# Attention stage of a hybrid encoder block: a hand-written pipeline of 100 slots on TensorE, ScalarE and VectorE, and keys' second halves copied by DMA

## The chip, the cores and the metric

The kernel runs on one core of a Trainium2 chip. A core has five engines that each work through their own queue: TensorE (PE; its weight loads are shown apart as PEld), VectorE (DVE), ScalarE (ACT), GpSimd (POOL) and SyncE (SP), which here issues nearly all DMAs. The metric is the device time of one execution in microseconds, lower is better. Three runs of the kernel before gave 1541.37, 1541.6 and 1543.32 us, median 1541.6 us.

## The reference, cut to what matters

One encoder block on 1024 positions of width 1024, all in float32:

```python
h = rmsnorm(x, g_mix) * (1 + scale1) + shift1
qa, ka, va, qb, kb, vb, ga, gb = split(h @ w_in)       # 6 x 512, 2 x 1024 columns
oa = mixture_of_dilations(qa, ka, va, rel_bias)        # 8 heads of 64, dilations 1, 4, 16
ob = neighbourhood_attention_2d(qb, kb, vb, na_rpb)    # 8 heads of 64, 16 x 64 grid, window 8 x 16
x = x + gate1 * ((sigmoid(ga) * (oa @ w_branch_dil) + sigmoid(gb) * (ob @ w_branch_na)) @ w_out)
h2 = rmsnorm(x, g_ffn) * (1 + scale2) + shift2
u_val, u_gate = split(depthwise_conv_seq(h2 @ w_up, conv_w, conv_b))
y = rmsnorm(x + gate2 * ((gelu(u_gate) * u_val) @ w_down), g_final)
```

Each attention is softmax(q k^T / 8 + bias) v with a window. In the dilated one, the three patterns are merged by their softmax denominators: the kernel computes a "near" pattern (dilation 1) and a "far" one (dilations 4 and 16 together, with the log of 2 where both apply) and weighs the two outputs per position.

## The kernel before, in words

**Stages.** The beginning (0 to about 160 us of the profile) makes `h`, the values of both branches and the adaLN sums. The attention stage (about 160 to 675 us) is the one that the change rewrites. Then follow the branch and output products (to about 860 us), the feed-forward up products (to about 1305 us) and down products (to the end).

**Splitting.** Float32 precision comes from splitting each operand into a high and a low part; a product of 512 columns over one block of 128 rows is three matmuls (`product`, L83 to L85: high x high, high x low, low x high). A weight tile of 128x1024 is loaded into `wraw` (`w_load`, L64), and `split` writes its high part on ACT (L56) and its low part on POOL (L60).

**Tiles of the attention stage.** 30 weight tiles are multiplied with `h`, each in two halves of 512 columns and 8 blocks of rows: 7 of queries, 7 of keys (the first pair's were done earlier) and 16 gate tiles. Each half lands in a PSUM bank `pj` (two buffers). Queries are evicted by `q_half` (L317 ACT, L318 DVE), keys by `k_half`: for each of the pair's two heads `i`, ACT writes the high part `ks` to the head's 64 partitions (L351), DVE the low part `kl` (L352), then ACT writes the high part a second time, to the other 64 partitions (L353), and POOL copies the low part there (L354). `gate_tile` evicts on ACT (L797) and writes to DRAM (`g_scr`, L798).

**Attention.** `attend_dil` takes a pair of heads: per head four far steps and four near steps of scores in PSUM `S` (two banks), a softmax (`softmax`: L606 DVE adds the bias and takes the maximum, L607 ACT exponent and sum), four transposes into PSUM `T` (two banks; L629, L667), a split of it into `th` and `tl` (L611 ACT, L612 DVE), and the product with the values into PSUM `O` (two banks; L636, L682), evicted by `finish_o` (L576, L577). After both heads follow the merging factors: 32 copies of a few elements on DVE (L692, L709), a spread of the factors to 128x512 on ACT (L713), transposes (L717) and the weighing (L719). `attend_na` does four column blocks per head: scores (L748), softmax (L752, L754), a normalisation on POOL and DVE (L759), transposes (L769), splits (L772, L773), products with the values (L781) and evictions (L787, L788). The results go to DRAM (`o_scr`, L724 and L789) and are read back by the next stage (`o_operands`, L842).

**What sets the order.** In this stage the program says only what is computed, pair after pair, with the next pair's projections and some gate tiles after each. A scheduler that runs a timeline of the engines at build time sets the order of every queue from that. Elsewhere `tc.manual_schedule(engines=...)` fixes the order of the named engines' instructions to the program's order; instructions outside of such a block can still be placed between them. The beginning up to the loads of the first two heads stands in such a block for all engines (SP's queue too), with the first pair's queries and keys made by a generator `qk_steps`; the stage after attention stands in another.

Of the kernel before, what the change touches and what calls it, by code (L numbers as in the profile page):

```python
# [28 lines left out]
def hybrid_encoder(tc, xT, c, w_ada, small, w_in, p1_bias, p23_bias, na_bias, ln2_mult, ident, w_br, w_out,  # L29
# [62 lines left out]
    qkpool = tc.alloc_tile_pool(name="qk", bufs=3)  # L92
# [29 lines left out]
    homes = iter([(qkpool, "kl", 3)] + [(qkpool, n, b) for n, b in (("qs", 3), ("ks", 3), ("qb", 2))  # L122
# [173 lines left out]
    def qk_steps(br, pr, ws=None, ps=None):  # L296
        qt, kt = ((0, 4), (12, 16))[br]
        qs = [qkpool.tile([128, S], FR, name="qs") for _ in range(2)]
        ks = [qkpool.tile([128, S], FR, name="ks") for _ in range(2)]
        kl = [qkpool.tile([128, S], FR, name="kl") for _ in range(2)]  # L300
        qb = []

        def q_half(hf, w, p=None):
            cols = halves[hf]
            if p is None:
                p = ps_g.tile([128, 512], FT, name="pj")
                if br == 0:
                    product(p, w, lambda k: h[hf, k])
                else:
                    q_windows(p, w, hf)  # L310
            for i in range(2):
                a, b = slice(64 * i, 64 * i + 64), slice(64 - 64 * i, 128 - 64 * i)
                d, pp = qs[i][:, cols], p
                if br:
                    d = qs[i].rearrange("p (v r t) -> p v r t", v=64, r=4)[:, :, 2 * hf:2 * hf + 2]
                    pp = p.rearrange("p (r v t) -> p v r t", r=2, v=64)
                act.activation(d[a], pp[a], AF.Copy)  # L317
                dve.tensor_tensor(d[b], pp[a], f(d[a]), OP.subtract)  # L318

        def q_windows(p, w, hf):  # L320

            whi, wlo = w
            for k in range(KT):
                mhi, mlo = (t.rearrange("p (r w c t) -> p r c w t", r=2, w=16, c=4) for t in h[hf, k])
                for x, (ww, m) in enumerate(((whi, mhi), (whi, mlo), (wlo, mhi))):
                    for r in range(2):
                        pe.matmul(p[:, 256 * r:256 * r + 256], ww[:, k], m[:, r], start=k + x + r == 0,
                                  stop=k == KT - 1 and x == 2, skip_group_check=True)

        def q_blocks():  # L330
            for i in range(2):
                q = qkpool.tile([128, S], FR, name="qb", bufs=2)
                for r in range(4):
                    pool.tensor_scalar(q.rearrange("p (b r j) -> p r b j", b=8, r=4)[:, r],
                                       f(qs[i][:, 256 * r:256 * r + 256]).rearrange("p (b j) -> p b j", b=8), 1.0, None,
                                       OP.mult)
                qb.append(q)

        def k_half(hf, w, p=None):
            cols = halves[hf]  # L340
            if p is None:
                p = ps_g.tile([128, 512], FT, name="pj")
                product(p, w, lambda k: h[hf, k])
            for i in range(2):
                a, b = slice(64 * i, 64 * i + 64), slice(64 - 64 * i, 128 - 64 * i)
                kh, ll, pp = ks[i][:, cols], kl[i][:, cols], p
                if br:
# [7 lines left out]

        if ws:
            for hf in range(2):
                yield
                if hf:
                    ps = [ps_g.tile([128, 512], FT, name="pj") for _ in range(2)]  # L360
                    for k in range(KT):
# [1151 lines left out]
```

## Time and profile before

| | us |
|---|---|
| median of three runs | 1541.6 |
| the profiled execution's own time | 1546.68 |
| its span, first to last instruction | 1544.9 |

The profile is of one execution, on the core's own clock. Its page gives the busy time of each engine, the span in 40 slices and the costliest groups; its views answer for a stretch of time ("windows"), for what an engine waited for ("waits"), or list the instructions in order of time ("timeline"). A matmul's row gives a start and a modelled duration; matmuls overlap, so that the distance from one start to the next is what one costs, and the busy share of PE says only where PE had nothing at all in flight. An "idle before" with an arrow names the instruction that ended the wait. SPq is SP's queue.

### The profile page before, as it was taken

The page shows a single profiled execution, that of the slowest core. Times are in us where ns is not written, and L with a number is a line of the kernel's source. Part 1 is how long each engine was busy: PE and PEld are TensorE (multiplying, and loading weights), DVE is VectorE, ACT ScalarE, POOL GpSimd, SP SyncE. Part 2 cuts the span into 40 slices and gives each one's busy share as a digit, 9 for nine tenths or more (in the row PEclk, how much of TensorE's full clock was granted, in tenths as well). Part 3 has the DMA queues.
Part 4 walks back from the last instruction along what each step waited for, and adds up shares of the span by engine and source line. Part 5 has one row for each costly group of instructions (what it writes and reads, how often), then busy time and mean ns, then how long its engine had stood idle before and what let it go on. Part 6 is the DMA issues. An engine that isn't in the chain of part 4 may idle for free. (4 is left out here: it accounts for less than half of the span.)

```text
span 1544.9 us, 21706 instructions
## 1 busy us (share of the span) xinstructions
PE 1502.2 (97%) x7740; PEld 1277.8 (83%) x7740; DVE 1005.9 (65%) x1884; ACT 802.1 (52%) x1440; POOL 815.6 (53%) x648
## 2 busy tenths in 40 slices
PE   8999999999999999999999898999999998999998
PEld 7988888888898898878888677888888887878787
DVE  6676457765766665536515898766666667787765
ACT  4331567675866767543345444444444447476442
POOL 1014355353537657312267678767777665778711
PEclk9999999999999999999999999999999999999998
DMA  9467232223534344467644112222222224513313
GB/s 349 174 255 249 67 93 66 89 74 88 159 97 134 117 140 136 156 207 230 205 152 153 49 69 96 82 82 83 84 88 88 84 79 166 200 52 134 105 55 110
DMA packets 108597, 196.86 MB, mean 127 GB/s; under 512 B 39716, under 2 KB 52388, under 8 KB 108452
## 3 DMA queue, kind: packets, MB, share of 16 engines
q1 hardware_dynamic: 108216, 195.20, 38.3%
q8 instruction: 61, 1.00, 0.3%
q14 instruction: 48, 0.39, 0.1%
q10 hardware_dynamic: 272, 0.26, 0.1%
HBM read 158.73 MB, written 42.47 MB: 130 GB/s over the span
## 5 line engine op out<-in xcount | busy, mean ns | idle before, releaser
L60 POOL TENSOR_TENSOR wlo<-wraw,whi 128x512 fp32r<-128x512 f32 (+1 forms) x154 | 193.4, 1277 | 247.1 <-ACT whi L56 234.6
L83 PE MATMUL pj<-h,whi 128*128 128x512 f32 x448 | 179.8, 401 | 3.8 <-ACT ks L353 1.8
L84 PE MATMUL pj<-h,whi 128*128 128x512 f32 x448 | 178.9, 399 | 1.6 <-DVE h L208 1.6
L85 PE MATMUL pj<-h,wlo 128*128 128x512 f32 x448 | 178.0, 397 | 0.0
L60 POOL TENSOR_TENSOR wsl<-big,wsh 128x512 fp32r<-128x512 f32 (+1 forms) x90 | 123.6, 1394 | 50.9 <-ACT wsh L56 50.9
L56 ACT ACTIVATE whi<-wraw 128x1024 fp32r<-128x1024 f32 (+2 forms) x81 | 81.1, 1002 | 81.9 <-PE pj L84 32.5
L354 POOL TENSOR_SCALAR kl<-kl 64x512 fp32r<-64x512 f32 x32 | 64.1, 2002 | 96.9 <-DVE kl L352 95.8
L1171 DVE SCALAR_TENSOR_TENSOR big<-wc,sm,big 128x256 f32<-128x256 f32 (+1 forms) x132 | 103.2, 830 | 16.8 <-ACT big L1165 16.6
L83 PEld LDWEIGHTS pj<-h,whi 128*128 128x128 f32 x448 | 84.9, 190 | 19.6 <-ACT ks L353 2.3
L606 DVE CUSTOM_DVE_ANT_0 P<-S,bias 128x256 f32<-128x256 f32 x128 | 52.0, 422 | 74.7 <-PE S L653 50.2
L84 PEld LDWEIGHTS pj<-h,whi 128*128 128x128 f32 x448 | 84.9, 190 | 17.0 <-DVE h L208 2.9
L85 PEld LDWEIGHTS pj<-h,wlo 128*128 128x128 f32 x448 | 84.9, 189 | 15.1
L607 ACT ACTIVATE P<-P,st 128x256 f32<-128x256 f32 x128 | 64.3, 503 | 40.0 <-DVE st L606 39.5
L1171 DVE SCALAR_TENSOR_TENSOR big<-pj,sm,big 128x512 f32<-128x512 f32 x132 | 67.1, 564 | 16.4 <-ACT big L1165 16.4
L60 POOL TENSOR_TENSOR wsl<-wraw,wsh 128x384 fp32r<-128x384 f32 (+1 forms) x46 | 53.8, 1190 | 44.8 <-ACT wsh L56 44.7
L1165 ACT ACTIVATE big<-wc,sm 128x512 f32<-128x512 f32 x44 | 35.8, 815 | 74.0 <-DVE wc L989 42.7
L563 POOL TENSOR_TENSOR vv<-vv 96x256 fp32r<-96x256 f32 (+2 forms) x32 | 41.0, 1289 | 59.2 <-ACT vv L562 54.6
L759 POOL TENSOR_SCALAR P<-P,stb 128x288 f32<-128x288 f32 (+1 forms) x32 | 39.2, 1226 | 48.0 <-DVE stb L756 41.1
L56 ACT ACTIVATE wsh<-big 128x1024 fp32r<-128x1024 f32 (+1 forms) x45 | 44.7, 997 | 37.2 <-POOL big L941 21.5
L1197 ACT ACTIVATE big<-big 128x1024 f32<-128x1024 f32 x22 | 23.3, 1060 | 74.6 <-DVE big L1171 74.6
L994 DVE TENSOR_TENSOR pj<-pj,wc 128x512 f32<-128x512 f32 x34 | 23.6, 695 | 58.3 <-PE pj L978 58.3
L612 DVE TENSOR_TENSOR tl<-T,th 128x512 fp32r<-128x512 f32 x64 | 43.9, 689 | 10.8 <-ACT th L611 10.1
(397 smaller groups left out, 4904.2 us busy)
## 6 DMA issues: line engine op xcount, KB each, us to landing
wraw<-w_in SPq DMA_DIRECT2D x34, 512.0 KB, 4.0
wada<-w_ada SPq DMA_DIRECT2D x31, 512.0 KB, 7.8
big<-w_up SPq DMA_DIRECT2D x22, 512.0 KB, 4.7
wraw<-w_up SPq DMA_DIRECT2D x22, 512.0 KB, 3.6
as<-big SPq DMA_DIRECT2D x22, 512.0 KB, 3.0
big<-as SPq DMA_DIRECT2D x22, 512.0 KB, 8.5
wraw<-w_down SPq DMA_DIRECT2D x24, 384.0 KB, 3.6
gs<-gs SPq DMA_DIRECT2D x32, 256.0 KB, 2.0
```

Of the source, the lines that this page charges most:

```text
L56: act.activation(hi, raw, AF.Copy)
L60: lo_eng.tensor_tensor(lo[:, i:i + step], raw[:, i:i + step], f(hi)[:, i:i + step], OP.subtract)
L83: pe.matmul(psum, whi[:, k0 + k], mhi, start=k == 0, stop=False)
L84: pe.matmul(psum, whi[:, k0 + k], mlo, start=False, stop=False)
L85: pe.matmul(psum, wlo[:, k0 + k], mhi, start=False, stop=k == n - 1)
L354: pool.tensor_scalar(ll[b], f(ll[a]), 1.0, None, OP.mult)
L563: pool.tensor_tensor(lo[:m, cs_], f(lo[:m, cs_]), f(vv[:m, cs_, 0:64]), OP.subtract)
L606: dve.tensor_tensor_reduce(pp, d, bias, -1.0, BIG, OP.add, OP.min, mi)
L607: act.activation(pp, pp, AF.Exp, bias=mi, scale=-1.0, accum_out=li)
L612: dve.tensor_tensor(tl, pt, f(th), OP.subtract)
L759: (pool, dve)[R].tensor_scalar(pp, pp, st[:, 1, 2 * cb + R:2 * cb + R + 1], None, OP.mult)
L1171: dve.scalar_tensor_tensor(y[:, dst], src, wt, y[:, dst], OP.mult, OP.add)
```

## The change

The functions `qk_steps`, `attend_dil`, `attend_na` and `gate_tile` go. In their place jobs are put into 101 slots (0 to 100), and one block with the order of PE, ACT and DVE fixed to the program's walks through the slots; POOL and SP are still ordered by the scheduler. A dilated head starts every 8 slots, a pair every 16, a neighbourhood head every 4 slots from slot 64 on. In each slot stand scores of one step, transposes of an earlier step and products with the values of a still earlier one, and between them `fill(n)` puts steps of the projections and gates (three matmuls of 512 columns each; 480 steps in all). Evictions and weight splits wait in a list `side`, and `catch_up` puts them behind each fill step up to a budget of 550 ns a step: first the ACT half, one step later the DVE half. `ensure(mark)` puts out what must stand before a given job. The walk through one slot:

```diff
+    with tc.manual_schedule(engines={e.engine for e in (pe, act, dve)}):
+        for s in range(101):
+            n = 4 if s < 64 else 8 if s < 72 else 6 if s < 88 else 4
+            run(slots[s]["first"])
+            run(slots[s]["O"])
+            fill(n // 4)
+            for job in run(slots[s]["T"]):
+                job()
+            fill(n // 4)
+            run(slots[s]["late O"])
+            run(slots[s]["S"])
+            run(slots[s]["last"])
+            fill(n - n // 4 * 2)
+            for job in run(slots[s]["W"]):
+                job()
+        for _ in range(60):
+            fill(4)
```

Where a head's jobs stand, and the list of side work:

```diff
+    class DilHead:
...
+            if self.head > 1:
+                at(s0 - 5, "first", self.load)
+            if s0:
+                at(s0 - 2, "first", self.prepare)
+                if pr:
+                    at(s0 - 4, "first", lambda: (ensure(qk_marks[pr]), q_blocks(qks[pr], i)))
...
+            for n in range(4):
+                at(s0 + n, "S", self.far_scores, n)
+                at(s0 + n + 2, "T", self.far_turn, n)
+                at(s0 + n + 3, "late O", self.far_out, n)
+                at(s0 + n + 4, "S", self.near_scores, n)
+                for js in (((0, 1),), ((2, 3),), ((4, 5),), ((6, 7), (8,)))[n]:
+                    at(s0 + n + 6, "W" if js == (8,) else "T", self.near_turn, js)
+                    at(s0 + n + 7, "late O", self.near_out, js)
...
+    class NaHead:
...
+            at(s0, "first", self.load)
+            at(s0 + 2, "last", self.prepare)
+            for n, cb in enumerate((0, 3, 1, 2)):
+                at(s0 + n - 1, "first", self.bias, cb)
+                at(s0 + n, "S", self.scores, cb)
+                at(s0 + n + 1, "first", self.normalise, cb)
+            for n, pair in enumerate(((0, 3), (1, 2))):
+                s = s0 + 3 + 2 * n
+                for y in range(3):
+                    at(s + (y == 2), "T", self.turn, pair, y)
+                at(s + 2, "O", self.out, pair)
...
+    def catch_up(ns):
+        flush()
+        credit[0] = min(credit[0], 0) + ns
+        while side and credit[0] > 0:
+            credit[0] -= emit()
```

The keys' second halves: ACT's second write and POOL's copy give way to DMAs on SP, four for each half of a dilated pair's keys, four for a whole neighbourhood pair:

```diff
-                act.activation(kh[a], pp[a], AF.Copy, scale=0.125)
-                dve.scalar_tensor_tensor(ll[a], pp[a], 0.125, f(kh[a]), OP.mult, OP.subtract)
-                act.activation(kh[b], pp[a], AF.Copy, scale=0.125)
-                pool.tensor_scalar(ll[b], f(ll[a]), 1.0, None, OP.mult)
...
+        def one():
+            for kh, ll, pp in parts:
+                act.activation(kh, pp, AF.Copy, scale=0.125)
+
+        def two():
+            for kh, ll, pp in parts:
+                dve.scalar_tensor_tensor(ll, pp, 0.125, f(kh), OP.mult, OP.subtract)
             for i in range(2):
                 a, b = slice(64 * i, 64 * i + 64), slice(64 - 64 * i, 128 - 64 * i)
...
+                for t in (qk[1][i], qk[2][i]):
+                    if br == 0:
+                        sp.dma_start(f(t)[b, halves[hf]], f(t)[a, halves[hf]])
+                    elif hf:
+                        sp.dma_start(f(t)[b], f(t)[a])
+        later(1500, one, two)
```

The first pair's keys take the same way: their DMAs stand in the beginning's block, in SP's fixed order, those of the second half just ahead of `va_chunks`. The spread of the merging factors goes from ACT to POOL, with a buffer of its own:

```diff
-                fw = sm_pool.tile([128, 4, 2, 64], FT, name="P", bufs=5)
-                act.activation(fw, fac[:, :, 4 * z:4 * z + 4].rearrange("p i b -> p b i")
-                               .rearrange("p b (i o) -> p b i o", o=1).to_broadcast([128, 4, 2, 64]), AF.Copy)
+            fw = self.fw[g, z] = at_pool.tile([128, 4, 2, 64], FT, name="fw")
+            pool.tensor_scalar(fw, self.fac[g][:, :, 4 * z:4 * z + 4].rearrange("p i b -> p b i")
+                               .rearrange("p b (i o) -> p b i o", o=1).to_broadcast([128, 4, 2, 64]), 1.0, None, OP.mult)
```

Query and key tiles get four buffers instead of three, so that two pairs have whole sets. The first weight split moves ahead of the last value products. Gate tiles stand as 2, 2, 2, 2, 2, 1, 1 and 4 beside the eight pairs instead of 2, 2, 2, 2, 1, 1, 0 and 6. In the stage behind attention, two PSUM names are allocated ahead of the others, so that the six banks of its `pj` no longer begin with banks of the gates' `pj`:

```diff
     ps = tc.alloc_tile_pool(name="ps", bufs=1, space=PSUM, reuse_waits="tile")
+    for name in ("pcol", "pbc"):
+        ps.tile([128, 512], FT, name=name)
```

The matmuls and transposes are the same in number and shape before and after; the near scores take their blocks in the order of the sequence, so that a head's near transposes come in groups of 3, 4, 4, 4 and 1.

700 lines of the change are left out of this document (406 added, 294 removed).

## Prediction

> **What bounds the kernel now.** I read the page first, then the attention stage in windows, then what TensorE waited for, then its instructions in order of time at the waits.
>
> ```profile
> span 1544.9 us, 21706 instructions
> ...
> PE 1502.2 (97%) x7740; PEld 1277.8 (83%) x7740; DVE 1005.9 (65%) x1884; ACT 802.1 (52%) x1440; POOL 815.6 (53%) x648
> ```
>
> TensorE has something in flight in 97% of the span, so no other engine can bound the whole. What the change can win lies in the part that it rewrites. The view of windows (columns: stretch, length, then busy time and count for PE, PEld, DVE, ACT, POOL, then granted clock, DMA share, GB/s):
>
> ```profile
> core 0: us, PE busy (x) PEld busy (x) DVE busy (x) ACT busy (x) POOL busy (x), PEclk, DMA share, GB/s
> 160.00:409.00 249.00, 245.40 (x1491) 215.91 (x1489) 158.86 (x469) 165.62 (x393) 106.21 (x85) 1.00 0.30 90
> 409.00:625.00 216.00, 212.63 (x1351) 191.09 (x1350) 137.69 (x360) 151.07 (x326) 129.99 (x97) 1.00 0.42 124
> 625.00:674.70 49.70, 49.62 (x264) 42.06 (x262) 21.63 (x41) 27.86 (x51) 10.57 (x8) 1.00 0.50 164
> 674.70:690.00 15.30, 11.74 (x45) 9.52 (x46) 6.18 (x9) 5.18 (x7) 2.51 (x2) 0.89 0.65 209
> 160.00:690.00 530.00, 519.39 (x3146) 458.57 (x3145) 324.37 (x879) 349.74 (x775) 249.27 (x191) 1.00 0.38 114
> ```
>
> From 160 to 690 us TensorE is idle for 530 - 519.39 = 10.6 us: 3.6 us in the dilated pairs, 3.4 us in the neighbourhood heads, 3.6 us at the passage to the next stage. The other engines are busy for at most 71% (ACT 151.07 of 216). So the stage is bound by TensorE's own work, and the prize is small. Who ended those waits (total us, times, longest), the first three of ten groups in the waits of PE between 150 and 690 us:
>
> ```profile
> PE pj L83 <- ACT gs L797: 3.6, 1, 3.6
> PE S L622 <- DVE st L606: 1.9, 2, 1.6
> PE pj L83 <- ACT ks L353: 1.8, 3, 1.2
> ```
>
> Scores wait for a softmax that must empty their bank, and projections wait for an eviction that ACT or DVE got to late. Each is a matter of order, not of work. The longest one in order of time:
>
> ```profile
> 674.00 0.39 PE L84 MATMUL pj<-h,whi 128*128 128x512 f32 x1
> 674.23 0.39 PE L85 MATMUL pj<-h,wlo 128*128 128x512 f32 x1
> 678.26 0.50 PE L83 MATMUL pj<-o0hi,whi 128*128 128x512 f32 x1 [3.65 <-ACT gs L797]
> ...
> 681.14 0.63 PE L83 MATMUL pj<-o0hi,whi 128*128 128x512 f32 x1
> 681.56 0.63 PE L84 MATMUL pj<-o0lo,whi 128*128 128x512 f32 x1
> ```
>
> The last gate matmul starts at 674.23 and the next stage's first at 678.26: its bank is one of the gates' own, and ACT empties that late.
>
> **The most that can be won.** A matmul of 512 columns costs 0.23 us from start to start (674.00 to 674.23). The wait shown as 3.65 us thus cost 4.03 - 0.23 = 3.80 us, since 0.15 us of it still counts as busy. The ten groups count 15 waits; with 0.15 us each, 10.6 + 15 x 0.15 = 12.9 us. Behind the longest one the clock fell (0.89 in its window), and matmuls were 0.42 us apart (681.14 to 681.56); eight such between 679.9 and 683.2 us add 8 x 0.19 = 1.5 us. Ceiling: 14.4 us, 0.9% of the time.
>
> The Trainium skill ("TensorE: Matmul & The Clock Gate", section "What's actually happening") says that an idle window of about 3.4 us puts TensorE's clock to one half. The trace agrees: 3.65 us of idleness, then 0.42 instead of 0.23 us.
>
> **The change, step by step.** *TensorE's work* is the same matmuls and transposes; grouping the transposes by four neither adds nor saves, by these rows:
>
> ```profile
> 165.89 0.82 PE L629 MATMUL T<-idt,P 128*128 128x128 f32 x6
> 166.46 0.48 PE L83 MATMUL pj<-h,whi 128*128 128x512 f32 x1
> 166.78 0.40 PE L84 MATMUL pj<-h,whi 128*128 128x512 f32 x1
> ...
> 171.88 0.28 PE L636 MATMUL O<-th,vv 128*128 128x256 f32 x1
> 172.00 0.28 PE L636 MATMUL O<-tl,vv 128*128 128x256 f32 x1
> ```
>
> Six transposes take 0.57 us and the matmul behind them 0.09 us more than 0.23, some 0.11 us each, much what 256 columns cost (0.12 us). Cost of the grouping: 0.
>
> The operations around it, in groups of the stretch from 160 to 690 us (count, then busy us and mean ns of one, then idle time ahead of them):
>
> ```profile
> L607 ACT ACTIVATE P<-P,st 128x256 f32<-128x256 f32 x126 | 63.3, 503 | 39.5 <-DVE st L606 39.0
> L606 DVE CUSTOM_DVE_ANT_0 P<-S,bias 128x256 f32<-128x256 f32 x126 | 51.2, 422 | 69.8 <-PE S L653 50.2 <-PE S L623 18.6
> L612 DVE TENSOR_TENSOR tl<-T,th 128x512 fp32r<-128x512 f32 x64 | 43.9, 689 | 10.8 <-ACT th L611 10.1
> L611 ACT ACTIVATE th<-T 128x512 fp32r<-128x512 f32 x64 | 37.2, 589 | 10.8 <-PE T L667 8.7 <-PE T L629 1.6
> L354 POOL TENSOR_SCALAR kl<-kl 64x512 fp32r<-64x512 f32 x28 | 57.6, 2056 | 45.3 <-DVE kl L352 44.1
> L353 ACT ACTIVATE ks<-pj 64x512 fp32r<-64x512 f32 x28 | 24.5, 875 | 11.1 <-DVE kl L352 10.8
> L713 ACT ACTIVATE P<-fx 128x512 f32<-128x512 f32 x8 | 5.0, 627 | 6.5 <-DVE fx L709 6.5
> ```
>
> *A slot.* Four fill steps of three matmuls are 4 x 0.69 = 2.8 us; four scores, four transposes and four or five value products at 0.11 to 0.12 us are 1.5 us. A dilated slot lasts 4.3 us. Scores of slot s are transposed in slot s+2, at least one slot and two fill steps later (5.7 us or more); in between come two maxima on DVE and two exponents on ACT (L606 and L607, 0.42 and 0.50 us each), about 2 us. From transposes to value products lies about one slot against 0.59 us on ACT and 0.69 us on DVE. The tightest place is the neighbourhood heads from slot 88 on: transposes, three fill steps and four scores, then the products, 2.6 us against 1.3 us plus what ACT holds ahead.
>
> ```profile
> L60 POOL TENSOR_TENSOR wlo<-wraw,whi 128x512 fp32r<-128x512 f32 (+1 forms) x154 | 193.4, 1277 | 247.1 <-ACT whi L56 234.6
> ```
>
> *Work off ACT and POOL.* The second halves leave ACT (24.5 us, and ACT's waits for DVE in the middle of an eviction, 10.8 us) and POOL (57.6 us). A key bank is free after ACT and DVE, without a third step: this is the wait "ACT ks" above. The spread leaves ACT (16 x 0.63 = 10 us) and comes to POOL, whose cost for it no row shows: bounds 1.3 us (its subtraction of 128x512, L60 above) to 2.1 us (its copy of 64x512, L354); I take 1.8, nearer to the copy, which has one operand like the spread; 16 x 1.8 = 29 us in 265 us of dilated slots, half of what leaves. None of this lies on TensorE's path while the other engines stay under 71%; if that cover were gone, a late softmax would hold the scores' bank and with it the queue behind them.
>
> *The waits.* All attention waits but the passage cost 12.9 - 3.8 = 9.1 us. The fixed order could leave 0 of it or bring back as much; the lead times above are two to three times the need, the tightest is not. I take 3 us left: won 6.
>
> ```profile
> 668.26 0.42 DVE L788 TENSOR_TENSOR u<-O,u 64x256 f32<-64x256 f32 x1
> ...
> 677.04 1.41 DVE L60 TENSOR_TENSOR o1lo<-oraw,o1hi 128x512 fp32r<-128x512 f32 x2 [3.17 <-ACT o1hi L56]
> ```
>
> *The passage.* The new banks do not wait for the last eviction, so the 3.8 us and the slow clock's 1.5 us go, unless the last head is late. Its last products stand in slot 99; 20 fill steps (13.6 us) and the first products (5 us) cover its way through DRAM, which in the trace takes from 668.7 (the last eviction's end) to 678.4 us (the last split's), 10 us. I take 1 us left: won 4.3.
>
> *The beginning.* Eight new DMAs stand in SP's fixed order there; the last four wait for DVE's `kl`, and behind them stand `va_chunks` and the row loads:
>
> ```profile
> 106.48 7.67 SPq L390 DMA_DIRECT2D v<-v  x4
> ...
> 118.32 5.14 SPq L133 DMA_DIRECT2D wada<-w_ada  x4
> ```
>
> ```profile
> 115.80 0.69 DVE L352 SCALAR_TENSOR_TENSOR kl<-pj,ks 64x512 fp32r<-64x512 f32 x1 [1.26 <-ACT ks L351]
> ...
> 128.96 7.07 DVE L494 SCALAR_TENSOR_TENSOR sq<-wada,cs,sq 128x512 f32<-128x512 f32 x6 [1.57 <-DMA wada<-w_ada]
> ...
> 139.97 2.33 DVE L494 SCALAR_TENSOR_TENSOR sq<-wada,cs,sq 128x512 f32<-128x512 f32 x3
> ```
>
> ```profile
> 149.23 0.95 PE L152 MATMUL pada<-ones,sq 128*128 128x1 f32 x8
> ```
>
> The row loads move from 118.3 to about 128 us, and DVE, which already waits for them at 128.96, runs some 9 us late. TensorE takes the last sum at 149.2 us, ready at 142.3 today: 7 us of slack, so 0 to 2 us lost. I take 0.5.
>
> **Sum.** 6 + 4.3 - 0.5 = 9.8, about 10 us off the profiled execution's 1546.68 us. The median run stands 5.1 us below it, so 1541.6 - 10 = 1531.6 us.
>
> **The rivals.**
>
> *A: the waits come back elsewhere.* Each queue keeps its order even where the next instruction could run; the order of before came out of a planned timeline and left only 9.1 us. If as much returns, the passage alone stays: 1541.6 - 4.3 + 0.5 = 1538 us. For it: DVE's peaks where a pair ends, when copies, weighing and a key eviction meet (some 4.5 us in a slot of 4.3). Against it: 65% mean load and leads of one slot.
>
> *B, the other side: SP's queue makes the softmax late.* POOL and SP are not fixed. A neighbourhood head's bias is loaded 1.3 slots before use into one of two buffers, and SP stands still behind evictions:
>
> ```profile
> SPq L798 <- ACT gs L797: 126.5, 30, 9.7
> ```
>
> ```profile
> bias<-na_bias SPq DMA_DIRECT2D x16, 384.0 KB, 3.2
> ```
>
> A bias load lands in 3.2 us; a slot from 64 on lasts 5 to 7.6 us, so a wait above some 4 us ahead of it makes DVE late, and DVE's fixed order then holds the splits and evictions behind it, and TensorE. The 30 waits average 4.2 us, at most 9.7. Up to 16 gate writes lie in those slots, and 12 key copies more wait on SP. With 1.2 us for each of 16: 19 us lost against 10 won, 1550 us. It decides from 0.6 us each.
>
> *C: all of the ceiling.* 1541.6 - 14.4 = 1527 us, if the written order leaves nothing.
>
> *D: the clock.* If many short waits pulled the clock down for a tenth of the stage, 53 us at half speed would cost 26 us: 1558 us. Against it stands the 1.00 of all windows before 674.7, with waits of up to 1.6 us in them. The Trainium skill ("TensorE: Matmul & The Clock Gate", section "A second HAM failure mode: psum-queue depth-cycling") tells of a kernel whose small idle times did this; no window of this trace shows it.
>
> **How the numbers follow.** My forecast, with its own range of 1527 to 1536: 0.49. C: 0.08. A: 0.2, two thirds of it still faster. B: 0.2. D: 0.03. About 0.2% (3 us) is what a measurement can tell from no change. Faster 0.49 + 0.08 + 0.12 = 0.69; same 0.08; slower 0.23. The range from 1524 to 1552 leaves out half of B, D and a little below C, under 0.2.
>
> **What would show it.** Right: TensorE's idle time from 160 to the next stage's first product falls from 10.6 to 3 to 5 us, no "ACT gs" wait at the passage, clock 1.00 there, the first `o0hi` matmul about 9 us earlier; no L353 and L354, SBUF copies on SP. Wrong: PE waiting for `th`, `tl` or DVE's maxima in many slots (A), DVE waiting for bias DMAs (B), a clock below 1.00 (D), or TensorE waiting at `pada` before 155 us (the beginning). A gain above 14.4 us would mean that TensorE's work itself got cheaper, which I rule out.

## The result, and the profile after

| | median us | runs | lowest to highest |
|---|---|---|---|
| before, beside the change | 1542.04 | 10 | 1540.63 to 1544.08 |
| after | 1539.69 | 10 | 1535.52 to 1542.53 |

The ratio is 0.9982, with a 95% interval of 0.9973 to 0.9992: 2.4 us are won, where 10 were forecast. By the bound set in the prediction (0.2%, about 3 us) that is no change that a measurement of this kernel tells well from none.

The page of the changed kernel, span and busy times:

```profile
span 1537.3 us, 21792 instructions
...
PE 1499.0 (98%) x7740; PEld 1270.1 (83%) x7740; DVE 996.0 (65%) x1892; ACT 770.4 (50%) x1437; POOL 775.8 (50%) x640
```

This span is 7.6 us below that of before, three times what the medians differ by. Most of the difference lies behind the attention stage. From the first product of the merged branches to the end of TensorE's work it was 770.1 us in the execution of before and 764.5 after, in stages that the change does not touch; in the other kernels of this study the same stretch took 763 to 768 us. There the granted clock stands at 0.50 for 23.6 us in before (887.9 to 891.2, 932.3 to 939.0, 1307.7 to 1314.5 and 1509.1 to 1515.9 us) and for 13.4 us in after (863.4 to 866.7, 883.9 to 890.6 and 1303.7 to 1307.1 us); 10 us more at half the clock are some 5 us by my estimate, nearly all of the 5.6. To judge the change I therefore use the stretch from the last value matmul of the beginning (`pv`) to the first product on `mhi`, the one fixed point behind the stage. Their rows, first of before, then of after:

```profile
159.71 0.39 PE L257 MATMUL pv<-vwh,h 128*128 128x512 f32 x1
...
768.01 0.39 PE L83 MATMUL pj<-mhi,whi 128*128 128x512 f32 x1
```

```profile
159.50 0.39 PE L258 MATMUL pv<-vwh,h 128*128 128x512 f32 x1
...
765.82 0.39 PE L84 MATMUL pj<-mhi,whi 128*128 128x512 f32 x1
```

608.3 us became 606.3: 2.0 us, as the medians say. The windows of after, with bounds that suit its own stages:

```profile
160.00:409.00 249.00, 247.48 (x1491) 213.97 (x1490) 153.45 (x474) 156.63 (x400) 103.48 (x90) 1.00 0.36 102
409.00:625.00 216.00, 212.96 (x1346) 190.45 (x1345) 128.43 (x345) 129.33 (x305) 96.06 (x82) 1.00 0.50 139
625.00:663.00 38.00, 35.82 (x209) 31.03 (x208) 23.07 (x56) 23.01 (x55) 14.63 (x13) 0.99 0.57 183
663.00:677.70 14.70, 14.70 (x62) 12.10 (x62) 6.02 (x11) 10.63 (x16) 2.54 (x2) 0.92 0.81 242
160.00:690.00 530.00, 523.25 (x3158) 457.74 (x3157) 316.68 (x893) 322.85 (x780) 219.25 (x188) 1.00 0.45 130
```

ACT fell from 349.7 to 322.9 us and POOL from 249.3 to 219.3, as the removed copies say. TensorE's idle time fell from 10.6 to 6.75 us, and a clock below 1.00 now stands inside the stage (0.92 from 663 to 677.7), where before it stood behind it. What TensorE waited for between 140 and 700 us (total, times, longest):

```profile
PE T L749 <- DVE tl L589: 1.9, 2, 1.7
PE O L932 <- DVE tl L589: 1.7, 5, 0.6
PE O L932 <- ACT th L588: 1.4, 1, 1.4
PE O L766 <- DVE tl L589: 0.9, 1, 0.9
...
PE pj L84 <- DVE kl L340: 0.4, 1, 0.4
...
```

The large groups of before are gone: no score waits for its softmax, no projection for `ks` or `qs`, and the passage's wait for `gs` is gone. In their place value products (0.6 us in before) and transposes wait for the split of the transposed weights (`th`, `tl`), and one projection waits 0.4 us for `kl`. But for 0.16 us at 390 us, behind a query eviction, those waits stand in two places. The first is at the evictions of neighbourhood keys, from 401 to 412 us and again, with at most 0.6 us each, at 470, 478, 535 and 586 us. The timeline at 412:

```profile
406.80 2.19 ACT L336 ACTIVATE ks<-pj 64x512 fp32r<-64x512 f32 x2
...
409.02 0.60 ACT L588 ACTIVATE th<-T 128x512 fp32r<-128x512 f32 x1
409.02 2.21 DVE L340 SCALAR_TENSOR_TENSOR kl<-pj,ks 64x512 fp32r<-64x512 f32 x2 [2.31 <-ACT ks L336]
...
411.26 0.69 DVE L589 TENSOR_TENSOR tl<-T,th 128x512 fp32r<-128x512 f32 x1
...
412.01 0.66 PE L749 MATMUL T<-idt,P 128*128 128x128 f32 x4 [1.70 <-DVE tl L589]
```

The two key writes stand in the fixed order ahead of the split, and each takes 1.1 us a head. ACT holds `th` back until 409.02, DVE holds `tl` until 411.26, the transposes' bank comes free late, and TensorE stands for 1.7 us.

The second place is the end, 650 to 661 us:

```profile
659.02 0.63 ACT L57 ACTIVATE o0hi<-oraw 128x512 fp32r<-128x512 f32 x1 [1.99 <-DMA oraw<-oa]
659.56 0.58 ACT L588 ACTIVATE th<-T 128x512 fp32r<-128x512 f32 x1
...
660.19 0.38 PE L932 MATMUL O<-th,vv 128*128 128x256 f32 x1 [1.39 <-ACT th L588]
...
661.03 0.39 PE L932 MATMUL O<-tl,vv 128*128 128x256 f32 x1 [0.46 <-DVE tl L589]
...
664.02 0.63 PE L86 MATMUL pj<-h,wlo 128*128 128x512 f32 x1
664.44 0.63 PE L84 MATMUL pj<-h,whi 128*128 128x512 f32 x1
```

`o0hi` is a split of the next stage's operand. It stands outside the fixed block, so it may be placed between the block's instructions, and here it was placed ahead of the last head's `th`. It waits 2 us for its rows from DRAM (`oraw`, four buffers), and `th` and TensorE wait with it. Behind these waits the clock fell (0.50 from 661.98 to 665.39 us): matmuls of 512 columns come 0.42 us apart at 664.

### The profile page after: what moved, and what is told of

It reads as the page before. It is cut to its first block, busy times and chain, and to the rows that moved or that the text cites. A ratio compares the mean times of both kernels' runs of the same rounds, so it can differ in the third digit from the quotient of the medians.

```text
span 1537.3 us, 21792 instructions
## 1 busy us (share of the span) xinstructions
PE 1499.0 (98%) x7740; PEld 1270.1 (83%) x7740; DVE 996.0 (65%) x1892; ACT 770.4 (50%) x1437; POOL 775.8 (50%) x640
## 5 line engine op out<-in xcount | busy, mean ns | idle before, releaser
L61 POOL TENSOR_TENSOR wlo<-wraw,whi 128x512 fp32r<-128x512 f32 (+1 forms) x96 | 118.3, 1253 | 172.9 <-ACT whi L57 139.1
L84 PE MATMUL pj<-h,whi 128*128 128x512 f32 x448 | 187.7, 419 | 1.8 <-ACT h L207 1.4
L85 PE MATMUL pj<-h,whi 128*128 128x512 f32 x448 | 177.8, 397 | 1.6 <-DVE h L209 1.6
L639 POOL TENSOR_TENSOR wlo<-wraw,whi 128x512 fp32r<-128x512 f32 x58 | 74.9, 1301 | 117.2 <-ACT whi L638 117.2
L589 DVE TENSOR_TENSOR tl<-T,th 128x512 fp32r<-128x512 f32 (+3 forms) x120 | 77.1, 653 | 72.9 <-ACT th L588 71.4
L1384 DVE SCALAR_TENSOR_TENSOR big<-wc,sm,big 128x256 f32<-128x256 f32 (+1 forms) x132 | 106.9, 859 | 16.1 <-ACT big L1378 15.9
L57 ACT ACTIVATE whi<-wraw 128x1024 fp32r<-128x1024 f32 (+2 forms) x52 | 50.7, 975 | 73.0 <-PE pj L85 27.6
L588 ACT ACTIVATE th<-T 128x512 fp32r<-128x512 f32 (+3 forms) x120 | 65.6, 566 | 20.3 <-PE T L919 14.0
L547 POOL TENSOR_TENSOR vv<-vv 128x512 fp32r<-128x512 f32 (+1 forms) x40 | 42.0, 1069 | 48.5 <-ACT vv L546 48.5
L580 DVE CUSTOM_DVE_ANT_0 P<-S,bias 128x256 f32<-128x256 f32 x128 | 48.9, 419 | 21.3 <-PE S L692 17.1
```

Source lines behind the costliest of these rows:

```text
L57: act.activation(hi, raw, AF.Copy)
L61: lo_eng.tensor_tensor(lo[:, i:i + step], raw[:, i:i + step], f(hi)[:, i:i + step], OP.subtract)
L84: pe.matmul(psum, whi[:, k0 + k], mhi, start=k == 0, stop=False)
L85: pe.matmul(psum, whi[:, k0 + k], mlo, start=False, stop=False)
L588: act.activation(th[:m, :n], pt[:m, :n], AF.Copy)
L589: dve.tensor_tensor(tl[:m, :n], pt[:m, :n], f(th)[:m, :n], OP.subtract)
```

## The experiments

Each kernel was timed in five rounds beside the kernel before; 0.1% is 1.5 us. "Stretch" is that from the last `pv` to the first `mhi` product in the profiled execution (before: 608.3). "Stalls" is a sum of mine over the same trace from the last `pv` to 25 matmuls into the next stage: distances from one matmul's start to the next, where they exceed the usual distance of that kind of matmul behind that kind of predecessor by over 60 ns (before: 16.9). It is of one execution, and sorting the kinds another way moves it by 1 us in most kernels and by 2 in before.

| kernel | median us | ratio to before | stretch | stalls |
|---|---|---|---|---|
| after | 1539.7 | 0.9982 (0.9973 to 0.9992) | 606.3 | 12.4 |
| b1_banks | 1538.1 | 0.9978 (0.9966 to 0.9989) | 602.5 | 11.2 |
| a1_nobanks | 1539.4 | 0.9988 (0.9976 to 1.0000) | 605.8 | 11.7 |
| a2_split | 1539.4 | 0.9987 (0.9976 to 0.9997) | 607.3 | 13.5 |
| a7_pace | 1538.4 | 0.9983 (0.9970 to 0.9995) | 606.4 | 12.6 |
| a3_late | 1542.0 | 1.0002 (0.9992 to 1.0013) | 607.1 | 11.4 |
| a6_raw8 | 1535.9 | 0.9960 (0.9947 to 0.9972) | 603.4 | 9.2 |
| a8_pace_raw8 | 1536.4 | 0.9963 (0.9949 to 0.9977) | 604.0 | 9.8 |
| b4_banks_raw8 | 1540.2 | 0.9994 (0.9983 to 1.0005) | 609.1 | 16.3 |
| a12_contig4 | 1532.4 | 0.9943 (0.9925 to 0.9962) | 602.1 | 8.2 |
| a10_contig | 1529.0 | 0.9926 (0.9910 to 0.9943) | 598.3 | 4.4 |
| b5_contig | 1541.6 | 1.0009 (0.9997 to 1.0020) | 607.6 | 16.4 |
| a11_rowkeys | 1536.9 | 0.9978 (0.9963 to 0.9994) | 603.3 | 3.7 |
| a4_copies | 1562.6 | 1.0144 (1.0125 to 1.0164) | 631.7 | 37.0 |
| b3_banks_dma | 1541.5 | 0.9996 (0.9985 to 1.0008) | 605.7 | 14.4 |
| b2_dma | 1547.5 | 1.0039 (1.0027 to 1.0051) | 609.2 | 17.7 |

### The two reserved banks

**b1_banks**: the kernel before with nothing but the two names.

```diff
     ps = tc.alloc_tile_pool(name="ps", bufs=1, space=PSUM, reuse_waits="tile")
+    for name in ("pcol", "pbc"):
+        ps.tile([128, 512], FT, name=name)
```

> The kernel before with nothing but the two PSUM names allocated first in the stage behind attention. Theory: the 3.65 us wait for the last gate eviction at the passage, and the slow clock behind it, are what the change really won, and they need no new order: the first product of the next stage moves from 678.3 to about 674.5 us, 4 to 5.3 us won, ratio to before 0.9966 to 0.9974, as good as the whole change or better. Rival: the operands of that product (the late splits of the last pair) or the banks of other names end the wait instead, and the ratio stays at 1.000.

Two lines alone give 0.9978, some 3.4 us, a little less than expected and as much as the whole change. By the stretch they are even 3.8 us better than the whole change; the medians don't confirm that, and the stretch is of one execution. The next stage's first product follows the gates' last one without a break, where before it came 4.03 us later:

```profile
673.00 0.39 PE L85 MATMUL pj<-h,wlo 128*128 128x512 f32 x1
673.23 0.39 PE L83 MATMUL pj<-o0hi,whi 128*128 128x512 f32 x1
673.45 0.39 PE L84 MATMUL pj<-o0lo,whi 128*128 128x512 f32 x1
```

**a1_nobanks**: the changed kernel with the same two lines taken out.

> The changed kernel without the two PSUM names first. Theory: a wait for the last gate eviction comes back at the passage, 2 to 5 us, ratio to before 1.000 to 1.002, so that the fixed order by itself wins nothing. Rival: in the changed kernel ACT gets to the last evictions early enough, the passage costs nothing either way and the ratio stays at 0.998.

The wait at the passage is back, 1.7 us of it (the next stage's first product 2.1 us behind the gates' last, not 0.23), yet the time is 0.9988, within the interval of the changed kernel and not the 1.000 to 1.002 expected. In its execution the wait for `th` at the end was 0.3 us, not 1.4, and its clock is 1.00 from 640 to 680 us, where after has 0.96: I read the two waits as one chain through the end of the stage, in which what one takes the other doesn't; that is argued, not tried. The order written out and the DMAs, without the banks, thus win 0.12% (0 to 0.24).

### The strided key writes

**a2_split** puts the two heads of a neighbourhood key eviction out as two pieces of side work, at 1100 ns each in place of 1500 for both; **a7_pace** does the same at 500 ns each.

```diff
-        later(1500, one, two)
+        if br == 0:
+            later(1500, lambda: one(parts), lambda: two(parts, range(2)))
+        else:
+            for i in range(2):
+                later(1100, lambda i=i: one(parts[i:i + 1]), lambda i=i: two(parts[i:i + 1], [i]))
```

> The changed kernel with the neighbourhood keys' eviction put into the list of side work head by head, in two pieces of 1.1 us per engine instead of one of 2.2. Theory: that lump stands ahead of the splits th and tl on ACT and DVE; TensorE's waits near 400 to 410, 469 to 478, 534 and 585 us, 5.3 us together, fall to under 2 us, and the ratio to before goes to 0.995 to 0.997. Rival: the lead between transposes and value products is too short whatever stands ahead, and the waits stay within 1 us of what they are (ratio 0.998).

> The changed kernel with the neighbourhood keys' eviction head by head as in a2_split, but at a price of 500 ns a piece in the list, so that one piece goes out with each fill step. Theory: a2_split took the lumps away (no wait left at 390 to 410 us) and gave 3.4 us back only because its price of 1100 ns put the second half's eviction behind its bank's next use; at 500 both are gone, the waits of TensorE from 380 to 640 us fall from 6.5 us in the changed kernel to under 2.5 us, ratio to before 0.996 to 0.998. Rival: the eviction's 2.2 us per engine must be paid somewhere in those slots, and the waits stay above 4 us.

Both miss: 0.9987 and 0.9983. In a2_split the waits from 390 to 412 us and at 478 us are gone, and one of the same size came, with the clock at 0.50 behind it (467.97 to 471.38 us), in the timeline of its profile:

```profile
464.31 1.06 ACT L336 ACTIVATE ks<-pj 64x512 fp32r<-64x512 f32 x1 [2.81 <-DVE kl L340]
...
467.34 1.06 DVE L340 SCALAR_TENSOR_TENSOR kl<-pj,ks 64x512 fp32r<-64x512 f32 x1
...
468.55 0.77 PE L84 MATMUL pj<-h,whi 128*128 128x512 f32 x1 [3.38 <-DVE kl L340]
```

In two pieces the eviction ends later, and now the projection's bank is what comes free late. In a7_pace the waits stayed about where they were in after (0.9 us at 397, 1.5 at 407 and 466, 0.6 at 474). Putting the lump elsewhere moves the wait at best; it doesn't remove it.

**a10_contig** takes the stride itself away, on top of eight row tiles (below): the keys are written in the order they come in. **a12_contig4** does it with the change's four row tiles, **b5_contig** in the kernel before. These three leave out that the neighbourhood keys are sorted into windows, so their scores are not the reference's; they only price the stride.

```diff
             if br:
-                kh, ll = (t.rearrange("p (w t r) -> p r w t", w=16, t=16)[:, 2 * hf:2 * hf + 2]
-                          for t in (qk[1][i], qk[2][i]))
-                pp = p.rearrange("p (r w t) -> p r w t", r=2, w=16)
+                pass
```

> The changed kernel with eight row tiles and with the neighbourhood keys of rows written in the order they come in, not in the order of their windows: the keys land in the wrong places, the instructions, their count, their order and all else stay. Theory 1: the strided write is what makes a piece take 1.1 us; contiguous, a piece takes 0.58 on ACT and 0.7 on DVE, the waits at 400, 405 and 410 us (3.3 us in all) go, and the kernel runs 2 to 3.5 us below the one with eight row tiles alone (1535.9), at 1532.5 to 1534. Rival: another lump (the weighing and copies of a pair's end) holds the thirds there, and the waits and the time stay.

> The changed kernel with only the neighbourhood keys written contiguous (in the wrong places), four row tiles as in the change. Theory 1: the waits behind the key evictions and those behind the next stage's splits are separate and their prices add: 7 us of the 10 between the changed kernel (1539.5) and the run with both (1529.0) belong to the keys, so 1532 to 1533.5 us. Rival: with the keys' lumps gone the heads run ahead of the row loads as well, and four row tiles do as well as eight: 1529 to 1530 us; or the splits' wait only grows to fill the gap: 1536 us.

> The kernel before with its neighbourhood keys written contiguous (in the wrong places), both halves: the two strided ACT writes of 1.1 us and the strided VectorE write become 0.58 and 0.7 us; order, banks and row tiles as before. Theory 1: the strided write is a price of any order, ACT and VectorE have 1 us less of a lump at each key column, and the waits of the matmuls behind ACT's and VectorE's key writes shrink: 2 to 4 us less, 1537 to 1539 us. Rival: the lumps hurt only where the order is fixed and the softmax stands behind them; the scheduler of before already places work around them, and the time stays within 1 us of 1541.

In the changed order the stride alone costs 0.9982 - 0.9943 = 0.39%, 6 us. The row of ACT's key write from a10_contig (durations: shortest, median, longest) reads

```profile
L334 ACT ACTIVATE ks<-pj x32: 571/592/596, 66.5 to 581.7; 64x512 fp32r<-64x512 f32 x32
```

where in the eight-row-tile kernel with strides it reads

```profile
L336 ACT ACTIVATE ks<-pj x32: 573/828/1106, 68.5 to 590.2; 64x512 fp32r<-64x512 f32 x32
```

With it every wait from 390 to 586 us went; what TensorE still waited for between 150 and 690 us in a10_contig:

```profile
PE pj L84 <- ACT gs L977: 0.6, 1, 0.6
PE T L917 <- DVE tl L587: 0.6, 1, 0.6
PE O L930 <- DVE tl L587: 0.3, 1, 0.3
```

a10_contig won more than expected (1529.0, not 1532.5 to 1534), since I had counted only the waits from 400 to 412 us and not the four later ones. In the kernel before, the same edit wins nothing (1.0009). That is the rival's time, but not its reason: the projections' waits for `ks` nearly went (1.8 to 0.2 us), as the theory had it, and the wait at the passage grew from 3.6 to 5.0 us:

```profile
PE pj L83 <- ACT gs L793: 5.0, 1, 5.0
```

**a11_rowkeys** asks for the gain with the keys in their right places: they are kept in the order of rows, and the score matmuls read windows of them with strides.

```diff
-            kv, lv = (t[self.i].rearrange("p (w c) -> p w c", w=16) for t in (ks, kl))
+            kv, lv = (t[self.i].rearrange("p (r w t) -> p w t r", r=4, w=16) for t in (ks, kl))
...
-                    pe.matmul(d, qs[self.i][:, qc], t[:, 4 * R:4 * R + 12, 4 * t0:4 * t0 + 4 * n], start=x_ == 0,
+                    pe.matmul(d, qs[self.i][:, qc], t[:, 4 * R:4 * R + 12, t0:t0 + n], start=x_ == 0,
```

> The changed kernel with eight row tiles and the neighbourhood keys kept in the order of their rows: the evictions write without strides, and the 128 score matmuls of the neighbourhood heads read their windows with strides instead (the same keys in the same order). Theory 1: TensorE reads a strided moving operand at the pace of a plain one, and the kernel keeps the time of the run with contiguous but misplaced keys, 1529 us (0.9926 of the kernel before). Rival: the strides cost the reader as much as they cost the writer (1.9 times: 64 matmuls of 384 columns at some 0.17 us and 64 of 288 at 0.13 would take 0.15 and 0.11 us more each, 17 us together), and the kernel runs near 1545 us.

Neither: 1536.9, between the two. Score matmuls of 384 columns, first in a10_contig, then in a11_rowkeys:

```profile
482.78 0.34 PE L895 MATMUL S<-ks,qs 128*128 128x384 f32 x1
482.96 0.34 PE L895 MATMUL S<-kl,qs 128*128 128x384 f32 x1
```

```profile
484.35 0.40 PE L895 MATMUL S<-ks,qs 128*128 128x384 f32 x1
484.57 0.40 PE L895 MATMUL S<-kl,qs 128*128 128x384 f32 x1
```

From start to start 0.18 us (482.78 to 482.96) became 0.22 (484.35 to 484.57); over the 64 of each size the mean went from 0.180 to 0.229 us, and for 288 columns from 0.132 to 0.169. That is 64 x 0.049 + 64 x 0.037 = 5.5 us, enough for the 5.0 us by which the stretch is longer (603.3 against 598.3). The waits are gone (3.7 us of stalls, 4.4 in a10_contig), but the stride is paid on the engine that bounds the stage.

### The next stage's splits

**a3_late** writes the eight `o0` splits out behind slot 99's products, each with two fill steps behind it. **a6_raw8** leaves the order alone and gives the rows eight buffers, and **a8_pace_raw8** is that with a7_pace. **b4_banks_raw8** is b1_banks with eight.

```diff
-                raw = opool.tile([128, 512], FT, name="oraw", bufs=4)
+                raw = opool.tile([128, 512], FT, name="oraw", bufs=8)
...
-            rows[n] = opool.tile([128, 512], FT, name="oraw", bufs=4)
+            rows[n] = opool.tile([128, 512], FT, name="oraw", bufs=8)
```

> The changed kernel with the splits of the next stage's first operand (o0) written into the fixed order behind the last head's products, two fill steps after each, instead of being placed by the scheduler between the last heads' work. Theory: the waits at 649 to 661 us and the slow clock behind them, 4.4 us together, go; if the splits still keep up with the 20 fill steps the ratio to before is 0.995 to 0.996, if they come late the passage takes back 2 to 5 us (0.998 to 1.000). Rival: these waits come from the short lead in the last slots (2.6 us), and they stay, at about 2.9 us, with the splits gone from between.

> The changed kernel with eight instead of four load buffers for the next stage's operands. Theory: the split that stands ahead of the last transposes' split waits for its DMA because only four loads are out at a time; with eight the scheduler's place for the splits is not changed into another engine's, but none waits, TensorE's waits at 656 to 661 us (2.3 us and the slow clock's 1.5) fall below 0.5 us, and from the last value product to the next stage's end 3 to 4 us are won on the changed kernel, ratio to before 0.995 to 0.997. Rival: the splits' own time (0.65 us each on ACT and on DVE) is what delays; the waits only move to an earlier transposition and the ratio stays at 0.998 to 0.999.

> Both a6_raw8 and a7_pace in one kernel. Theory: they are separate in time and add up; the stretch from the last value product of the beginning to the next stage's last product, 606.3 us in the changed kernel, falls to 599 to 601 us, ratio to before 0.993 to 0.996, the fastest so far. Rival: a fixed order pushes each wait to the next place, and the stretch stays above 603 us.

> The kernel before with the two banks reserved and with eight row tiles for the output projection, its order of work left as it was. Theory 1: the eight row tiles won 3.5 us in the changed kernel (1539.4 to 1535.9) because there the splits of the next stage stood among the last heads and waited for their rows; the kernel before has no such splits among its last heads, so here they win nothing, and the kernel runs at the 1538 us of the banks alone (0.998 of the kernel before). Rival: the row tiles also end a wait at the entry of the output projection whatever the order, and the kernel runs at 1535 us or less (0.996 or lower), so that the hand-written order is worth nothing at all.

a3_late wins nothing (1.0002). Its waits from 649 to 661 us are gone and its first `o0` product starts at 671.5, but the splits of the second branch, `o1`, are then late, and the clock is 0.50 behind their waits (680.46 to 683.87 us). The timeline of its profile:

```profile
676.95 0.50 PE L84 MATMUL pj<-o1hi,whi 128*128 128x512 f32 x1 [0.56 <-ACT o1hi L57]
...
679.16 0.50 PE L84 MATMUL pj<-o1hi,whi 128*128 128x512 f32 x1 [0.76 <-ACT o1hi L57]
```

a6_raw8 wins 0.22% on the changed kernel (0.9960). Its splits run early and in one piece, and the last head's `th` doesn't wait; the timeline of its profile:

```profile
648.55 3.75 ACT L57 ACTIVATE o0hi<-oraw 128x512 fp32r<-128x512 f32 x7
```

With a8_pace_raw8, which can't be told from it, it is the fastest kernel that computes all of the reference: 5.2 us below the kernel before in its own call, 1541.06 to 1535.91 us. Its clock is 1.00 from 640 to 680 us, where after has 0.96. a8_pace_raw8 adds nothing to it, where 0.993 to 0.996 was expected. In the order of before the eight buffers win nothing on top of the banks; a wait of 2.9 us for `o1hi` came at 679.8 us in b4_banks_raw8:

```profile
679.78 0.80 PE L83 MATMUL pj<-o1hi,whi 128*128 128x512 f32 x1 [2.95 <-ACT o1hi L56]
```

So the banks and the buffers without the written order and the DMAs come to 0.9994, and with them to 0.9960. The edits don't add up over orders.

### The key copies by DMA

**a4_copies** is the changed kernel with ACT's second write and POOL's copy back in place of the DMAs. **b2_dma** is the kernel before with the DMAs alone, **b3_banks_dma** that with the banks.

```diff
             for kh, ll, pp in parts:
                 act.activation(kh, pp, AF.Copy, scale=0.125)
+            for (kh, ll, pp), kb in zip(parts, others):
+                act.activation(kb[0], pp, AF.Copy, scale=0.125)
```

> The changed kernel with the keys' second halves written as before: a second ACT write (0.54 to 0.83 us a piece, four pieces a key column of 1024) and a Pool copy, in place of the DMA copies. Theory 1: the strided second write makes the ACT lump of a neighbourhood key eviction 4.4 us in place of 2.2, so that the waits of value products and transposes behind it grow: 1541 to 1546 us. Rival: ACT has room there and the DMA copies were worth nothing, 1539 us as the changed kernel.

> The kernel before with the two PSUM names first and the keys' second halves copied by DMA, but with the scheduler's own order. Theory: a key eviction without its third step frees the bank earlier and takes away most of the waits ended by the second key write and its neighbours (2.6 us in the kernel with the banks alone), ratio to before 0.996 to 0.9975, against 0.9978 with the banks alone. Rival: the scheduler lays out a different order whose waits are as many, ratio 0.9975 to 0.999.

> The kernel before with only the DMA copies of the keys' second halves, no banks, its scheduler's order otherwise. Theory 1: by the run with both (1541.5 against 1538.1 with the banks alone) the DMA copies cost the scheduler's order 3.4 us, and alone they give 1543 to 1546 us. Rival: that loss came from the way the scheduler placed things in that one build, and alone the copies give 1541 us or less, since ACT and Pool have less to do.

a4_copies shows the largest effect of the study: 1.0144, 25 us above the changed kernel, far above the 1541 to 1546 us expected. The timeline of its ACT and DVE:

```profile
411.62 2.20 ACT L338 ACTIVATE ks<-pj 64x512 fp32r<-64x512 f32 x2
413.83 2.19 ACT L340 ACTIVATE ks<-pj 64x512 fp32r<-64x512 f32 x2
416.04 0.60 ACT L587 ACTIVATE th<-T 128x512 fp32r<-128x512 f32 x1
```

```profile
416.05 2.17 DVE L344 SCALAR_TENSOR_TENSOR kl<-pj,ks 64x512 fp32r<-64x512 f32 x2 [4.29 <-ACT ks L340]
418.26 0.69 DVE L588 TENSOR_TENSOR tl<-T,th 128x512 fp32r<-128x512 f32 x1
```

The lump on ACT is 4.4 us as expected; what I missed is that DVE's write stands behind all of it, so `tl` comes 6.6 us after the eviction began, and stalls are three times those of after. Part of them is the clock: it stands at 0.50 in five places of the stage (406.35 to 409.76, 420.00 to 423.40, 481.44 to 484.80, 549.70 to 556.50 and 607.74 to 611.10 us), 20 us in all, of which half, some 10 us, is lost by my estimate. With the copies placed so, both ACT writes ahead of DVE's, the fixed order thus loses; other places for them were not tried. In the order of before the DMAs lose: 0.9996 against 0.9978 with the banks, 1.0039 against 1 without. In both builds with DMAs in that order one 2.8 us wait of a score matmul is new, and in b3_banks_dma the rows of DVE and POOL ahead of it are

```profile
461.86 3.26 DVE L762 TENSOR_SCALAR P<-P,stb 128x384 f32<-128x384 f32 x1
465.05 0.45 DVE L755 CUSTOM_DVE_ANT_0 P<-S,bias 128x288 f32<-128x288 f32 x1
```

```profile
462.43 2.48 POOL L726 TENSOR_TENSOR u<-u,u 128x512 f32<-128x512 f32 x2
```

A normalisation of this size takes DVE 0.56 us on average in the changed kernel (0.44 for 288 columns). Here it took 3.26, and ended 0.2 us behind POOL's two operations; in b2_dma one took 3.27, from 463.88 us, and ended 0.2 us behind two such operations as well. Two more things differ from before in both. TensorE waits at `pada` for DVE's `ada` (1.4 us at 145.31 us in b2_dma, 1.5 at 143.36 in b3_banks_dma). And the clock is 0.50 behind that wait (147.6 to 151.0, 144.2 to 147.6 us) and behind the score's (468.5 to 471.8, 465.1 to 471.8 us). What each of them costs was not tried.

## Why the prediction was wrong, by its own steps

**The waits: the step that failed.** "I take 3 us left: won 6." In the trace of after, TensorE idles for 1.52 + 3.04 + 2.18 = 6.7 us from 160 to 677.7 us, and with 0.15 us for each of the 11 waits 8.4 us are left of 9.1. The sum missed the stretch by 9.8 - 2.0 = 7.8 us; 5.3 of them lie in this step, which won 9.1 - 8.4 = 0.7 and not 6, and 2.4 in TensorE's own work (below). The step was right that the large waits of before would go: they did. It was wrong in holding the leads ("two to three times the need") against a normal load on ACT and DVE. Where those two queues are in fixed order, what counts is the longest thing that stands ahead of a split. It said so itself for "the tightest place", the neighbourhood heads from slot 88 on, but gave no figure for "what ACT holds ahead" there. The waits at the very end lie in these slots (slot 88 starts at about 608 us), behind splits that it didn't count; those from 401 to 412 us came among the last dilated slots, which it didn't single out. Two things stood in the text and were not put together. The trace of before showed key writes of 875 and 915 ns on average, a mean over contiguous ones of 0.58 and strided ones of 1.1, and the change's list prices an eviction of four such writes (two on each engine) at 1500 ns, while the trace has 2.2 on ACT and then 2.2 on DVE. And the description of the kernel had it that instructions outside a fixed block can be placed between those of the block, but the next stage's splits were not looked for there. The experiments price the two at 6 us (a12_contig4) and 3.4 us (a6_raw8), together 8.6 (a10_contig). With both away the kernel stands 11.4 us below that of before, by 0.9926. So the forecast of 10 us fits an order without these items; a10_contig gets there only by leaving the keys unsorted.

The Trainium skill (SBUF — State Buffer, note on cachelines under "Door 1: The DMA port swizzle") says that accesses that each go to a new line of 16 bytes pay for it. The trace agrees: key writes 16 bytes apart take 1.1 us, and contiguous ones 0.59.

**The passage: right, and its clock half wrong.** The 3.65 us wait is gone, the first `o0hi` product follows 0.23 us behind the gates' last (b1_banks shows that the banks do this), and the last head was not late there. The slow clock's 1.5 us came back 15 us earlier, behind the waits at 658.5 to 661 us: six matmuls of 512 columns from 663.06 to 665.58 took 2.5 us in place of 1.4, and six value products ahead of them 0.3 us more than usual. Won: about 3.9 of the 4.3.

**TensorE's work: not free.** The grouping of transposes costs nothing, as said. But even without the stalls the same matmuls stand further apart: my sum of the other distances is 508.7 us before and 511.1 after, and 511.4 in a6_raw8 (with the kinds sorted another way, after is 1.7 us above before). Half a microsecond of it belongs to four score matmuls that before has done earlier. What makes up the other 2 us was not tried.

**The beginning: right, and 0 for 0.5.** DVE's sums start at 135.13, 6 us later than before, and the last of them ends at 146.44; TensorE's next use of them starts at 149.03, without a wait (before: 149.23).

```profile
144.11 2.33 DVE L475 SCALAR_TENSOR_TENSOR sq<-wada,cs,sq 128x512 f32<-128x512 f32 x3
```

**The spread** on POOL took 1.49 us, within the bounds of 1.3 and 2.1.

The sum as measured: 0.7 + 3.9 - 2.4 + 0 = 2.2 us, against 2.0 in the stretch.

**The rivals.** A, "the waits come back elsewhere", came true, at 1539.7 us where it had 1538, by another place than the one argued for it (lumps of strided writes and foreign splits, not the copies where a pair ends). B: neither a bias load nor SP's queue is among what TensorE or DVE waited for. C did not come. D: no window in the heart of the stage is below 1.00; the slow clock stayed at one place. It did come in a4_copies, whose waits are longer, at five.

## What to carry to other kernels

When an order is written out by hand, list the longest single items of each fixed queue with their durations by shape, not their means, and put each beside the lead of what stands behind it. A truer price for such an item didn't help here (a2_split); taking its stride away did. Look also at what is free to slip into the fixed block from the next stage. And try the smallest edits of a large change alone: here two lines alone won as much as the whole, and the DMA copies, much better than the copies by ACT and POOL in one order, lost time in the other.

## What the runs showed of the hardware

- A write of 64x512 from PSUM with elements 16 bytes apart took 1.1 us on ACT and on DVE, a contiguous one 0.59 and 0.7. A matmul that reads its moving operand with strides (innermost step 1 KB) took 1.28 times as long from start to start (0.229 against 0.180 us for 384 columns, 0.169 against 0.132 for 288). The writers, at their step of 16 bytes, took 1.9 times as long on ACT and 1.6 on DVE.
- The clock fell behind waits of 1.39 and 0.46 us that lay within 2.5 us of each other, not only behind one long one: 0.42 us per matmul of 512 columns at 664. The Trainium skill (TensorE: Matmul & The Clock Gate, "What's actually happening") speaks of an idle window of about 3.4 us. Here no such window was idle throughout. The slow stretches of these traces last 3.41 us or twice that, so I count in steps of 3.41 us from their starts. In the 3.41 us ahead of the slow stretch (658.57 to 661.98) TensorE was busy for 1.57 us, and in before, ahead of its own (676.22 to 679.63), for 1.37. The single wait of 1.70 us at 412 left 1.71 us of work in its 3.41 us (409.40 to 412.81), and the clock stayed at 1.00. So several pieces of idle time, about half of such a stretch together, went ahead of the slow clock. A limit can't be read from this: b2_dma was busy for 2.19 of the 3.3 us from 144.2 to 147.5 us and had 0.50 behind them.
- A DVE `TENSOR_SCALAR` from SBUF to SBUF took 3.26 us beside two POOL operations that ended 0.2 us earlier, against 0.56 on average in the changed kernel; in b2_dma the same happened once more (3.27 us). That the POOL operations held it is argued from the rows, not tried.
